# Strassen's seven products in three of five column groups of each feed-forward layer, with the sums of weights on GpSimd

## The chip, the cores and the metric

One core of a Trainium2 chip runs the whole program in one launch. The metric is the device time in microseconds, the median of several runs. The engines are TensorE (PE in the rows, its weight loads PEld), VectorE (DVE), ScalarE (ACT), GpSimd (POOL) and SyncE (SP), which here issues the weight transfers.

## The reference, cut to what matters

Two blocks of a transformer over 256 tokens of 1024 features, in float32, have three feed-forward layers of the same shape, with 2816 hidden columns:

```
def swiglu(h, w1, w3, w2):
    return (jax.nn.silu(h @ w1) * (h @ w3)) @ w2      # h [256, 1024], w1 and w3 [1024, 2816], w2 [2816, 1024]
```

The second block's layer is the same with other names (w_ffn_gate, w_ffn_up, w_ffn_down). `h` is the normed input; the kernel multiplies by the norm's factor of a row only after the product. The change touches `h @ w1` and `h @ w3`, which this document calls the first projections.

## The kernel before, in words

**Products.** A float32 product is made of three passes on TensorE: each operand is split into a high and a low part of 12 bits, and high*high, high*low and low*high are summed in PSUM (`mm3`, L196 to L198). The normed tokens stand still, 128 of them by 128 features at a time (`n["hi"]`, `n["lo"]`, tiles xT_hi and xT_lo), and 512 columns of weights move past them.

**Weights.** All weights go once through SBUF, in the order of use (`Stream`). A load brings 2048 words of each partition (1 MB: four chunks of 128 rows by 512 columns) into one of four w_raw buffers, by a transfer that SP issues. A piece is half a load: two chunks of 128 rows by 512 columns. For each piece ScalarE makes the high part (L141, w_raw to w_hi) and VectorE the low part (L142, w_raw less w_hi, to w_lo); both inputs of L142 lie in SBUF. `advance` keeps `AHEAD = 4` pieces split ahead of the one in use, and there are five buffers for each part.

**The feed-forward layer** (`ffn`, L410). The 2816 columns are cut in five groups of 512 and one of 256. A group calls `proj` for w1 and then for w3. Each `proj` takes four pieces; with each piece it makes six matrix instructions for the first 128 tokens and six for the others, into two PSUM banks. So a group has 8 pieces and 96 matrix instructions. When a bank is full, `gate` (L433, ScalarE, silu from PSUM to sg) or `up` (L438, VectorE, PSUM times factor times sg, to hid) empties it. Then `turn` transposes hid on TensorE, eight blocks of 128 by 128 in two parts, and each part is split to hT_hi (L204, ScalarE) and hT_lo (L205, VectorE) for the last projection (`outproj`, L362), which comes after all groups.

**Order.** The order of each engine's work is that in which the Python program issues it. Side work are generators; a `tick` comes after every six large matrix instructions and runs what is due (`turn` waits 2 ticks before each of its parts), then calls `advance`. `finish` ticks until given tasks are done. GpSimd has only the small steps of the norms and of head factors (`inv_sqrt`, L225 to L230, on tiles of 1 to 8 columns, `norm_s`, L261) and four copies (L729).

Of the kernel before, what the change touches and what calls it, by code (L numbers as in the profile page):

```python
# [23 lines left out]
F32 = mybir.dt.float32  # L24
# [5 lines left out]
P = 128  # L30
# [24 lines left out]
# columns of the constants, in three parts (always needed, first block, second block)  # L55
# [5 lines left out]
# Ticks that the tensor engine's share of a task waits for the other engines' (see Kernel.spawn).  # L61
# [48 lines left out]
class Stream:  # L110
    """Weights in the order of their use: loads run ahead, splits run ahead of the products."""

    def __init__(self, nc, raw, hi, lo, ahead_load, ahead_split):
        self.nc, self.raw_p, self.hi_p, self.lo_p = nc, raw, hi, lo
        self.al, self.asp = ahead_load, ahead_split
        self.slots, self.pieces = [], []
        self.raws, self.parts = {}, {}
        self.i = self.loaded = self.split = 0

    def add(self, w, k0, kc, c0, n):  # L120
        """Rows k0*P .. (k0+kc)*P of w, n columns from c0: one load, split by as many row chunks as a piece holds."""
        self.slots.append((w, k0, kc, c0, n))
        step = PIECE // n
        for k in range(0, kc, step):
            self.pieces.append((w, k0 + k, min(step, kc - k), c0, n, len(self.slots) - 1, k))

    def _load(self, i):
        w, k0, kc, c0, n = self.slots[i]
# [4 lines left out]
        self.raws[i] = v  # L133

    def _split(self, i):
        nc = self.nc
        w, k0, kc, c0, n, slot, k = self.pieces[i]
        raw = self.raws[slot][:, k * n:(k + kc) * n]
# [4 lines left out]
        self.parts[i] = (hi.rearrange("p (k n) -> p k n", n=n), lo.rearrange("p (k n) -> p k n", n=n))  # L143

    def advance(self, limit=10 ** 9):
        want = min(len(self.pieces) - 1, self.i + self.asp - 1, limit)
        slot = min(len(self.slots), self.pieces[min(self.i, len(self.pieces) - 1)][5] + self.al)
        while self.loaded < max(slot, self.pieces[want][5] + 1):
            self._load(self.loaded)
            self.loaded += 1  # L150
        while self.split <= want:
            self._split(self.split)
            self.split += 1

    def take(self, w, k0, c0):
        if self.i not in self.parts:
            self.advance()
        spec = self.pieces[self.i]
        assert spec[0] is w and spec[1] == k0 and spec[3] == c0, (spec[1:], k0, c0)
        got = self.parts.pop(self.i)  # L160
        self.i += 1
        return spec[2], got


class Kernel:
    def __init__(self, ctx, tc, a, out):
# [3 lines left out]
        self.raw = pool("raw", 4)  # L170
# [21 lines left out]
    def mm3(self, out, a, b, start=False, stop=False):  # L192
        """out += a.T @ b, both split."""
# [6 lines left out]
    def evac_split(self, hi, lo, src, scale=None):  # L200
        """hi + lo = src * scale."""
# [8 lines left out]
    def split(self, hi, lo, src):  # L210
        """hi + lo = src, all in SBUF."""
# [7 lines left out]
    def inv_sqrt(self, out, ss, n, eps, width):  # L219
        """out = (ss / n + eps) ** -0.5"""  # L220
# [19 lines left out]
    def norm_piece(self, n, gcol, h, c):  # L240
        """x * g, transposed and split, for half h of the tokens and half c of the features; its squares' sum."""
# [27 lines left out]
    # Work beside the large products: generators, that yield after how many ticks to go on. A tick comes after  # L269
    # every six large products, so what a task asks of the other engines is done when the tensor engine needs it.  # L270
# [852 lines left out]
```

## Time and profile before

| what | value |
|---|---|
| median of three runs | 1030.45 us (1028.41 to 1030.77) |
| profiled execution, span | 1027.8 us |
| PE busy | 1013.2 us, 99% |
| DVE busy | 628.4 us, 61% |
| ACT busy | 546.8 us, 53% |
| POOL busy | 64.1 us, 6% |
| mean DMA rate | 170 GB/s |

The span runs from the first to the last instruction of the profiled execution; its own time with what lies around the span isn't given apart, and the median of the runs is 2.65 us above the span. The page gives each engine's busy time, then the chain of work that ended last: what each step waited for, followed back from the last instruction. Busy time of PE counts pipelined instructions, so the rate is read from starts, not from durations.

### The profile page before, as it was taken

The page shows a single profiled execution, that of the slowest core. Times are in us where ns is not written, and L with a number is a line of the kernel's source. Part 1 is how long each engine was busy: PE and PEld are TensorE (multiplying, and loading weights), DVE is VectorE, ACT ScalarE, POOL GpSimd, SP SyncE. Part 2 cuts the span into 40 slices and gives each one's busy share as a digit, 9 for nine tenths or more (in the row PEclk, how much of TensorE's full clock was granted, in tenths as well). Part 3 has the DMA queues.
Part 4 walks back from the last instruction along what each step waited for, and adds up shares of the span by engine and source line. Part 5 has one row for each costly group of instructions (what it writes and reads, how often), then busy time and mean ns, then how long its engine had stood idle before and what let it go on. Part 6 is the DMA issues. An engine that isn't in the chain of part 4 may idle for free.

```text
span 1027.8 us, 13120 instructions
## 1 busy us (share of the span) xinstructions
PE 1013.2 (99%) x5126; PEld 846.9 (82%) x5126; DVE 628.4 (61%) x892; ACT 546.8 (53%) x820; POOL 64.1 (6%) x167
## 2 busy tenths in 40 slices
PE   7999999999999999999999999999999999999998
PEld 6887888898888998788888888888887888888886
DVE  5977655554475877655555466666677665555542
ACT  7666545443366776644444366675444464444431
POOL 2320000000010000200000015000020010000000
PEclk9999999999999999999999999999999999999999
DMA  9543655555555323465655545355534546555541
GB/s 308 179 140 106 217 193 170 199 168 201 164 198 170 106 100 104 140 202 172 202 169 190 176 163 205 124 194 171 198 123 167 182 145 226 181 195 175 183 144 42
DMA packets 82638, 174.50 MB, mean 170 GB/s; under 512 B 2960, under 2 KB 19984, under 8 KB 82576
## 3 DMA queue, kind: packets, MB, share of 16 engines
q1 hardware_dynamic: 82288, 173.57, 49.9%
q8 instruction: 40, 0.66, 0.3%
q14 instruction: 22, 0.18, 0.1%
q10 hardware_dynamic: 288, 0.09, 0.0%
HBM read 172.60 MB, written 1.05 MB: 169 GB/s over the span
## 4 chain that ended last, share of the span: by engine, by line
PE 93%; DVE 3%; POOL 2%; issue 1%; ACT 1%; DMA 1%; SPq 0%; DVEq 0%; ACTq 0%
PE acc L362 27%; PE acc L196 18%; PE acc L198 18%; PE acc L197 18%; PE misc L217 4%; PE z L196 1%; POOL is_y L226 1%; PE z L198 1%; PE z L197 1%; PE misc L197 1%; DMA x<-in_x_dram 1%; PE misc L196 1%; PE misc L198 1%; PE z L821 1%; PE z L807 0%
## 5 line engine op out<-in xcount | busy, mean ns | idle before, releaser
L142 DVE TENSOR_TENSOR w_lo<-w_raw,w_hi 128x1024 fp32r<-128x1024 f32 (+1 forms) x323 | 392.7, 1222 | 301.2 <-ACT w_hi L141 300.8
L141 ACT CAST w_hi<-w_raw 128x1024 fp32r<-128x1024 f32 (+1 forms) x323 | 337.3, 1050 | 354.8 <-PE acc L198 228.5
L196 PE MATMUL acc<-w_hi,xT_hi 128*128 128x512 f32 (+2 forms) x1008 | 372.1, 370 | 0.0
L197 PE MATMUL acc<-w_lo,xT_hi 128*128 128x512 f32 (+2 forms) x1008 | 366.7, 364 | 0.0
L198 PE MATMUL acc<-w_hi,xT_lo 128*128 128x512 f32 (+2 forms) x1008 | 366.5, 364 | 0.0
L198 PEld LDWEIGHTS acc<-w_hi,xT_lo 128*128 128x128 f32 x1008 | 190.2, 189 | 30.3
L196 PEld LDWEIGHTS acc<-w_hi,xT_hi 128*128 128x128 f32 x1008 | 190.3, 189 | 29.1 <-ACT xT_hi L207 0.9
L197 PEld LDWEIGHTS acc<-w_lo,xT_hi 128*128 128x128 f32 x1008 | 190.5, 189 | 28.0
L362 PE MATMUL acc<-w_lo,hT_hi 128*128 128x512 f32 x264 | 104.6, 396 | 0.0
L362 PE MATMUL acc<-w_hi,hT_hi 128*128 128x512 f32 x264 | 104.4, 395 | 0.0
L362 PE MATMUL acc<-w_hi,hT_lo 128*128 128x512 f32 x264 | 86.7, 395 | 0.0
L362 PEld LDWEIGHTS acc<-w_hi,hT_hi 128*128 128x128 f32 x264 | 49.8, 189 | 11.3
L362 PEld LDWEIGHTS acc<-w_hi,hT_lo 128*128 128x128 f32 x264 | 49.7, 188 | 11.3
L362 PEld LDWEIGHTS acc<-w_lo,hT_hi 128*128 128x128 f32 x264 | 49.7, 188 | 11.1
L261 POOL TENSOR_TENSOR norm_s<-norm_ss 128x1 f32<-128x1 f32 x12 | 3.8, 313 | 611.8 <-ACT junk L257 611.8
L208 DVE SCALAR_TENSOR_TENSOR xT_lo<-misc,gains,xT_hi 128x128 fp32r<-128x128 f32 (+1 forms) x84 | 28.0, 353 | 22.6 <-ACT xT_hi L207 22.5
L207 ACT ACTIVATE xT_hi<-misc,gains 128x128 fp32r<-128x128 f32 (+1 forms) x84 | 29.0, 371 | 11.5 <-DVE xT_lo L208 9.0
L433 ACT ACTIVATE sg<-acc,norm_rstd 128x512 f32<-128x512 f32 (+1 forms) x36 | 23.6, 655 | 18.1 <-PE acc L198 17.9
L396 DVE TENSOR_TENSOR x<-acc,x 128x512 f32<-128x512 f32 x24 | 16.5, 690 | 14.1 <-PE acc L362 13.7
L438 DVE SCALAR_TENSOR_TENSOR hid<-acc,norm_rstd,sg 128x512 f32<-128x512 f32 (+1 forms) x36 | 23.9, 700 | 0.5 <-PE acc L198 0.5
L226 POOL TENSOR_TENSOR is_y<-is_v,mhalf 128x1 f32<-128x1 f32 (+2 forms) x24 | 23.8, 993 | 2.0
L257 ACT ACTIVATE junk<-x 128x512 f32<-128x512 f32 x24 | 15.2, 632 | 16.4 <-DVE x L396 14.7
(266 smaller groups left out, 973.8 us busy)
## 6 DMA issues: line engine op xcount, KB each, us to landing
w_raw<-in_ffn_w_dram SPq DMA_DIRECT2D x66, 1024.0 KB, 5.0
w_raw<-in_w_in_dram SPq DMA_DIRECT2D x26, 1024.0 KB, 5.0
w_raw<-in_od_w_qkv_dram SPq DMA_DIRECT2D x12, 1024.0 KB, 5.2
w_raw<-in_w_ffn_gate_dram SPq DMA_DIRECT2D x11, 1024.0 KB, 5.1
w_raw<-in_w_ffn_up_dram SPq DMA_DIRECT2D x11, 1024.0 KB, 5.0
w_raw<-in_w_ffn_down_dram SPq DMA_DIRECT2D x11, 1024.0 KB, 4.8
w_raw<-in_ev_w_in_dram SPq DMA_DIRECT2D x5, 1024.0 KB, 7.8
w_raw<-in_ev_w_out_dram SPq DMA_DIRECT2D x4, 1024.0 KB, 7.0
```

Source lines behind the costliest of these rows:

```text
L141: nc.scalar.copy(hi, raw)
L142: nc.vector.tensor_sub(lo, raw, hi.bitcast(F32))
L196: nc.tensor.matmul(out, ah, bh, start=start, stop=False, skip_group_check=True)
L197: nc.tensor.matmul(out, ah, bl, start=False, stop=False, skip_group_check=True)
L198: nc.tensor.matmul(out, al, bh, start=False, stop=stop, skip_group_check=True)
L207: nc.scalar.mul(hi, src, scale)
L208: nc.vector.scalar_tensor_tensor(lo, src, scale, hi.bitcast(F32), op0=OP.mult, op1=OP.subtract)
L217: self.nc.tensor.transpose(out, in_, self.ident)
L226: nc.gpsimd.tensor_tensor(y, v, self.mhalf[:, :width], op=OP.pow)
L362: mm = lambda a, b, start, stop: self.nc.tensor.matmul(o, a, b, start=start, stop=stop, skip_group_check=True)
L433: nc.scalar.activation(s[:, :m], acc[:, :m], AF.Silu, scale=n["rstd"][:, h:h + 1])
L438: nc.vector.scalar_tensor_tensor(t[:, :m], acc[:, :m], n["rstd"][:, h:h + 1], sg[h][:, :m], op0=OP.mult, op1=OP.mult)
```

## The change: what it does

The two projections of one group are one product: the tokens' matrix, cut in four quarters (two halves of 128 tokens by two halves of 512 features), times a matrix with 512 columns of w1 on the left and the same 512 of w3 on the right, also in four quarters of 512 rows by 512 columns (b11, b12, b21, b22). Before, that took eight products of quarters. In three groups of each layer (the second, third and fifth) it now takes seven, in Winograd's arrangement of Strassen's scheme: x1 = a11 b11 and w = a12 b21, whose sum is the upper left quarter of the result, one product of a sum of tokens with b22 as it lies, one of a22 with a sum of weights, and three of sums with sums. Each product takes two pieces and twelve matrix instructions. A group so has 14 pieces and 84 matrix instructions, where it had 8 and 96.

The sums of weights are made on GpSimd (`_sum`): four for a group, each an addition of two tiles of 128 by 2048 words. The first three take a buffer of a pool of two (w_sum), the fourth is written over the second. A sum may be issued up to 12 pieces ahead of its use, if its sources have been issued as loads or sums and a buffer is free. The sums of tokens (`token_sums`) are made once for a layer, after its first group, on VectorE with copies on ScalarE, from xT_hi and xT_lo. Products add up in PSUM where they can; where a partial sum is used twice, ScalarE copies the bank (`snap`), and VectorE adds or subtracts (`result`).

The weight loads have five buffers in place of four, and a load is issued as soon as the load five before it has been split and summed. In the retention layer the split scores lie in other tiles, and head 3 waits for head 0's end. All else in the diff is comments.

```
+RING = 5
+SUMS = 2
+SUMS_AHEAD = 12
...
+    def add_block(self, wl, cl, wr, cr):
+        h = KD // 2
+        b11 = self._load_of(wl, 0, h, cl, 512)
+        b12 = self._load_of(wr, 0, h, cr, 512)
+        b22 = self._load_of(wr, h, h, cr, 512)
+        b21 = self._load_of(wl, h, h, cl, 512)
+        s1 = self._sum_of(b11, b12)
+        s2 = self._sum_of(s1, b22)
+        s3 = self._sum_of(b12, b22)
+        s4 = self._sum_of(s2, b21, over=True)
+        for q, src in ((1, b11), (2, b21), (5, s1), (6, s2), (3, b22), (7, s3), (4, s4)):
+            for k in range(0, h, 2):
+                self._piece(src, k * 512, 2, 512, (wl, q, k, cl))
...
+    def _may_load(self):
+        j = self.loaded
+        return j < len(self.loads) and (j < self.ring or self.loads[j - self.ring]["users"] == 0)
...
+    def _sum(self):
...
+            s["tile"] = self.sum_p.tile([P, SLOT], F32, name="w_sum")
...
+        self.nc.gpsimd.tensor_tensor(s["tile"], x["tile"], y["tile"], op=OP.add)
...
+    FF_GROUPS = ((0, 512, False), (512, 512, True), (1024, 512, True), (1536, 512, False), (2048, 512, True), (2560, 256, False))
...
+    def token_sums(self, n, pool, tmp, out):
...
+        def difference(dst, x, y):
+            nc.vector.tensor_sub(dst, f(*x, "hi"), f(*y, "hi"))
+            nc.vector.tensor_sub(e, f(*x, "lo"), f(*y, "lo"))
+            nc.vector.tensor_add(dst, dst, e)
+
+        def done(which, src):
+            hi, lo = out[which]
+            nc.scalar.copy(hi, src)
+            nc.vector.tensor_sub(lo, src, hi.bitcast(F32))
+
+        difference(s, (1, 0), (1, 1))
+        done(5, s)
+        yield 2
+        nc.vector.tensor_sub(s, s, f(0, 0, "hi"))
+        nc.vector.tensor_sub(s, s, f(0, 0, "lo"))
+        done(6, s)
+        yield 2
+        nc.vector.tensor_add(s, s, f(0, 1, "hi"))
+        nc.vector.tensor_add(s, s, f(0, 1, "lo"))
+        done(3, s)
+        yield 2
+        difference(d, (0, 0), (1, 0))
+        done(7, d)
+
+    def block(self, n, sums, wl, c0, wr, snap, result):
...
+                    self.mm3(acc, left[q](k + kk), (wh[:, kk], wl_[:, kk]), start=start and k + kk == 0, stop=k + kk == KD // 2 - 1)
+                if k + kc < KD // 2:
+                    self.tick()
...
+        x = self.ps_acc()
+        product(x, 1, True)
+        after(snap, "x1", x)
+        w = self.ps_acc()
+        product(w, 2, True)
+        after(result, 0, 0, w)
+        z = self.ps_acc()
+        product(z, 5, True)
+        after(snap, "z", z)
+        product(x, 6, False)
+        after(snap, "x2", x)
+        product(z, 3, False)
+        after(result, 1, 0, z)
+        product(x, 7, False)
+        after(snap, "x3", x)
+        v = self.ps_acc()
+        product(v, 4, True)
+        after(result, 0, 1, v)
...
+                def snap(what, acc):
+                    nc.scalar.copy(home[what], acc)
+                    if what == "x3":
+                        nc.vector.tensor_sub(hid[1], hid[1], sg[1])
+
+                def result(side, h, acc):
+                    if side == 0:
+                        nc.vector.tensor_add(sg[h], acc, sg[h])
+                        nc.scalar.activation(sg[h], sg[h], AF.Silu, scale=n["rstd"][:, h:h + 1])
+                    else:
+                        nc.vector.tensor_sub(hid[h], acc, hid[h])
+                    if side == 1 or h == 1:
+                        nc.vector.scalar_tensor_tensor(hid[h], hid[h], n["rstd"][:, h:h + 1], sg[h], op0=OP.mult, op1=OP.mult)
...
+            for c0, m, block in self.FF_GROUPS:
+                if block:
+                    self.finish([made])
+                hid = by_block(c0) if block else plain(c0, m)
+                if not made:
+                    made = self.spawn(self.token_sums(n, f2, lambda i: f2.tile([P, 512], F32, name=("sg0", "sg1", "hid0")[i]), sums))
                 last = self.spawn(turn(c0, m, hid))
...
             def ret_head(j):
+                while j >= 3 and rets[j - 3] in self.live:
+                    yield 1
...
-                sh = se2.tile([P, 384], F32R, name="ret_sh")
-                sl = se2.tile([P, 384], F32R, name="ret_sl")
+                sh, sl = splits[j % 3]
```

## Rows read from the trace of the kernel before

**Rows 1.** The profile's page: busy time by engine; chain that ended last, by engine.

```profile
PE 1013.2 (99%) x5126; PEld 846.9 (82%) x5126; DVE 628.4 (61%) x892; ACT 546.8 (53%) x820; POOL 64.1 (6%) x167
...
PE 93%; DVE 3%; POOL 2%; issue 1%; ACT 1%; DMA 1%; SPq 0%; DVEq 0%; ACTq 0%
```

**Rows 2.** Busy time by stretch: first projections of the three layers, columns named above.

```profile
core 0: us, PE busy (x) PEld busy (x) DVE busy (x) ACT busy (x) POOL busy (x), PEclk, DMA share, GB/s
...
98.60:224.20 125.60, 125.60 (x621) 106.02 (x621) 71.86 (x77) 63.50 (x81) 2.07 (x7) 1.00 0.58 193
...
419.50:545.00 125.50, 125.50 (x619) 104.88 (x619) 71.01 (x79) 63.15 (x83) 3.36 (x8) 1.00 0.55 185
...
836.50:962.30 125.80, 125.80 (x623) 106.21 (x622) 72.25 (x78) 62.79 (x79) 2.06 (x7) 1.00 0.57 193
```

**Rows 3.** The same view, one group of 512 columns, between two starts of L438.

```profile
165.87:188.61 22.74, 22.74 (x105) 18.80 (x105) 12.32 (x13) 10.66 (x12) 0.00 (x0) 1.00 0.56 184
```

**Rows 4.** Timeline of PE, 163 to 168 us (start, duration); instructions follow one another.

```profile
164.80 0.39 PE L196 MATMUL acc<-w_hi,xT_hi 128*128 128x512 f32 x1
...
167.97 0.39 PE L198 MATMUL acc<-w_hi,xT_lo 128*128 128x512 f32 x1
```

**Rows 5.** Instruction groups by shape, 143.14 to 188.61 us: busy us, mean ns, idle before.

```profile
L142 DVE TENSOR_TENSOR w_lo<-w_raw,w_hi 128x1024 fp32r<-128x1024 f32 x17 | 20.8, 1225 | 22.3 <-ACT w_hi L141 22.3
L141 ACT CAST w_hi<-w_raw 128x1024 fp32r<-128x1024 f32 x16 | 16.8, 1053 | 22.2 <-PE acc L198 22.2
...
L438 DVE SCALAR_TENSOR_TENSOR hid<-acc,norm_rstd,sg 128x512 f32<-128x512 f32 x4 | 2.8, 744 | 0.0
L433 ACT ACTIVATE sg<-acc,norm_rstd 128x512 f32<-128x512 f32 x4 | 2.8, 690 | 1.9 <-PE acc L198 1.9
L205 DVE TENSOR_TENSOR hT_lo<-misc,hT_hi 128x512 fp32r<-128x512 f32 x4 | 2.7, 684 | 0.0
...
L204 ACT CAST hT_hi<-misc 128x512 fp32r<-128x512 f32 x4 | 2.3, 579 | 0.0
```

**Rows 6.** Instruction groups of DVE over the span: 128x512, both inputs in SBUF.

```profile
L976 DVE TENSOR_TENSOR a<-a,b 128x512 f32<-128x512 f32 x4 | 2.7, 682 | 0.0
```

**Rows 7.** Timeline of DVE, 48 to 58 us.

```profile
48.43 1.22 DVE L142 TENSOR_TENSOR w_lo<-w_raw,w_hi 128x1024 fp32r<-128x1024 f32 x1
...
51.95 1.22 DVE L142 TENSOR_TENSOR w_lo<-w_raw,w_hi 128x1024 fp32r<-128x1024 f32 x1
53.09 0.74 DVE L208 SCALAR_TENSOR_TENSOR qT<-misc,gq,qT 128x512 fp32r<-128x512 f32 x1
53.75 2.35 DVE L142 TENSOR_TENSOR w_lo<-w_raw,w_hi 128x1024 fp32r<-128x1024 f32 x2
```

**Rows 8.** Timeline of POOL, the same stretch.

```profile
48.60 1.10 POOL L225 TENSOR_SCALAR is_v<-hn_ss 128x8 f32<-128x8 f32 x1 [5.92 <-DVE hn_ss L454]
49.79 1.64 POOL L226 TENSOR_TENSOR is_y<-is_v,mhalf 128x8 f32<-128x8 f32 x1
...
52.07 1.15 POOL L229 TENSOR_SCALAR is_t<-is_t 128x8 f32<-128x8 f32 x1
53.31 0.20 POOL L230 TENSOR_TENSOR rq<-is_t,is_y 128x8 f32<-128x8 f32 x1
...
53.88 3.71 POOL L226 TENSOR_TENSOR is_y<-is_v,mhalf 128x8 f32<-128x8 f32 x1
```

**Rows 9.** Instruction groups of POOL, 28 to 33 us.

```profile
L729 POOL CAST vp<-vp 128x128 fp32r<-128x128 f32 x3 | 0.9, 292 | 9.5 <-ACT vp L207 9.2 <-DVE vp L208 0.3
```

**Rows 10.** Instruction groups of POOL, 603 to 606 us.

```profile
L228 POOL TENSOR_TENSOR is_t<-is_t,is_v 128x1 f32<-128x1 f32 x1 | 0.2, 191 | 0.1
```

**Rows 11.** Instruction groups of POOL, 626 to 628 us.

```profile
L228 POOL TENSOR_TENSOR is_t<-is_t,is_v 128x8 f32<-128x8 f32 x1 | 0.2, 204 | 0.1
```

**Rows 12.** Timeline of DVE, 176 to 190 us, the end of a group.

```profile
187.47 1.22 DVE L142 TENSOR_TENSOR w_lo<-w_raw,w_hi 128x1024 fp32r<-128x1024 f32 x1 [1.49 <-ACT w_hi L141]
188.61 1.40 DVE L438 SCALAR_TENSOR_TENSOR hid<-acc,norm_rstd,sg 128x512 f32<-128x512 f32 x2
```

More of the change, by code (lines that the diff above doesn't have):

```diff
@@ L110, with __init__ @@
 class Stream:
-    def __init__(self, nc, raw, hi, lo, ahead_load, ahead_split):
+    def __init__(self, nc, raw, hi, lo, ring, sum_ring, ahead_split, ahead_sum):
         self.nc, self.raw_p, self.hi_p, self.lo_p = nc, raw, hi, lo
[L115 to L118, printed above, removed]
+        self.sum_p = None
+        self.ring, self.sum_ring, self.asp, self.asum = ring, sum_ring, ahead_split, ahead_sum
+        self.loads, self.sums, self.pieces = [], [], []
+        self.buffers = []
+        self.parts = {}
+        self.taken = 0
+        self.i = self.loaded = self.summed = self.split = 0
@@ new lines, in _source, with _load_of, _sum_of @@
+    def _source(self, **kw):
+        return dict(users=0, tile=None, **kw)
+    def _load_of(self, w, k0, kc, c0, n):
+        s = self._source(spec=(w, k0, kc, c0, n), words=kc * n)
+        self.loads.append(s)
+        return s
+    def _sum_of(self, x, y, over=False):
+        s = self._source(xy=(x, y), words=x["words"], first=None, over=over, heir=None)
+        x["users"] += 1
+        y["users"] += 1
+        if over:
+            x["heir"] = s
+        else:
+            self.buffers.append(s)
+        self.sums.append(s)
+        return s
@@ L129, in _load @@
+    def _load(self):
+        s = self.loads[self.loaded]
+        w, k0, kc, c0, n = s["spec"]
         t = self.raw_p.tile([P, SLOT], F32, name="w_raw")
@@ L132, in _load, with _may_sum, _split @@
                                w[k0 * P:(k0 + kc) * P, c0:c0 + n].rearrange("(k p) n -> p k n", p=P))
-        self.raws[i] = v
-    def _split(self, i):
+        s["tile"] = v
+        self.loaded += 1
+    def _may_load(self):
+        j = self.loaded
+        return j < len(self.loads) and (j < self.ring or self.loads[j - self.ring]["users"] == 0)
+    def _may_sum(self):
+        j = self.summed
+        if self.sum_p is None or j >= len(self.sums) or any(x["tile"] is None for x in self.sums[j]["xy"]):
+            return False
+        s = self.sums[j]
+        if s["over"]:
+            return s["xy"][0]["users"] == 1
+        if self.taken < self.sum_ring:
+            return True
+        last = self.buffers[self.taken - self.sum_ring]
+        while last["users"] == 0 and last["heir"] is not None:
+            last = last["heir"]
+        return last["users"] == 0
+    def _sum(self):
+        s = self.sums[self.summed]
+        x, y = s["xy"]
+        if s["over"]:
+            s["tile"] = x["tile"]
+        else:
+            s["tile"] = self.sum_p.tile([P, SLOT], F32, name="w_sum")
+            self.taken += 1
+        self.nc.gpsimd.tensor_tensor(s["tile"], x["tile"], y["tile"], op=OP.add)
+        x["users"] -= 1
+        y["users"] -= 1
+        self.summed += 1
+    def _split(self):
         nc = self.nc
-        w, k0, kc, c0, n, slot, k = self.pieces[i]
-        raw = self.raws[slot][:, k * n:(k + kc) * n]
+        src, off, kc, n, key = self.pieces[self.split]
+        raw = src["tile"][:, off:off + kc * n]
         hi = self.hi_p.tile([P, PIECE], F32R, name="w_hi")[:, :kc * n]
@@ new lines, in block, with product, after @@
+    def block(self, n, sums, wl, c0, wr, snap, result):
+        plain = lambda k0, h: lambda k: tuple(n[p][:, k0 + k, h * P:(h + 1) * P] for p in ("hi", "lo"))
+        summed = lambda i: lambda k: tuple(t[:, k] for t in sums[i])
+        left = {1: plain(0, 0), 2: plain(4, 0), 4: plain(4, 1), **{i: summed(i) for i in (3, 5, 6, 7)}}
+        def product(acc, q, start):
+            for k in range(0, KD // 2, 2):
+                kc, (wh, wl_) = self.st.take(wl, q, k, c0)
+                for kk in range(kc):
+                    self.mm3(acc, left[q](k + kk), (wh[:, kk], wl_[:, kk]), start=start and k + kk == 0, stop=k + kk == KD // 2 - 1)
+                if k + kc < KD // 2:
+                    self.tick()
+        def after(f, *args):
+            self.run(f(*args))
+            self.tick()
+        x = self.ps_acc()
[16 more added lines that the diff above has]
+        after(result, 0, 1, v)
@@ L425, in turn, with plain @@
                     self.evac_split(hh[:, k:k + 2, :], hl[:, k:k + 2, :], tp.rearrange("p (k t) -> p k t", t=T))
-            for c0 in range(0, FF, 512):
-                m = min(512, FF - c0)
+            def plain(c0, m):
                 sg, hid = [], []
```

93 lines of the change are left out of this document (63 added, 30 removed).

## Prediction, on record before the changed kernel ran

> **What bounds the kernel now.** I read the page first: PE is busy 99% of the span and makes 93% of the chain that ended last, DVE 3% [rows 1]. So PE's stream of matrix instructions sets the time, and POOL is nearly free (64.1 us). Next the stretches: the first projections of the three layers take 125.6, 125.5 and 125.8 us, PE busy throughout, the granted clock 1.00, its higher level (2.4 GHz) [rows 2]. Then one group of 512 columns: 22.74 us, in which DVE is busy 12.32 and ACT 10.66 us [rows 3]. The reader is to see that this slack, some 10 us of DVE, belongs to a group of 8 pieces. Last the PE timeline: 15 matrix instructions start between 164.80 and 167.97 us, so 3.17 / 14 = 0.2264 us apart [rows 4]; 96 of them are 21.74 us, and the other 1.0 us of the group is the eight transposes.
>
> **What PE saves.** 12 instructions fewer in each of nine groups: 12 x 0.2264 = 2.72 us a group, 24.5 us in all. A changed group costs PE 84 x 0.2264 + 1.0 = 20.0 us.
>
> **What DVE gets.** A changed group has 14 pieces where there were 8, and each wants one L142 and one L141. On DVE, by rows 5 for the same kinds and rows 6 for two inputs in SBUF: 14 x 1.225 = 17.15; two additions and one subtraction from PSUM, 3 x 0.684 = 2.05 (as L205); the subtraction after x3, 0.68; two products as L438, 2 x 0.744 = 1.49; two L205, 1.37. Together 22.7 us in 22 instructions. Instructions back to back overlap a little: two L142 take 2.35 us, so the second adds 1.13 and not 1.22 [rows 7], and L438 starts 1.14 us after L142 [rows 12]. Less 0.09 for each: 20.8 us. ACT: 14 x 1.053 + four copies and two casts of turn at 0.579 + two silus at 0.690 = 19.6 us [rows 5]. So even alone DVE takes 20.8 us of a group of which PE wants 20.0: the cover of rows 3 is gone, because a piece now feeds six instructions (1.36 us) where it fed twelve. Only 1.9 us a group could be won against 22.74.
>
> **Sums of tokens.** After the first group of a layer DVE makes 14 instructions of 128 x 512 with both inputs in SBUF: 14 x (0.682 - 0.08) = 8.4 us [rows 6], and in each of the four `done` it waits for ACT's copy, about 0.6 us (0.579 in rows 5): 10.8 us in all. They stand on DVE ahead of the split of piece 5 of the next group. PE has four pieces ahead (4 x 1.36) and the transposes (1.0), 6.4 us, and then waits.
>
> **Second and third group together, without GpSimd in the way.** From the end of the first group DVE has: its last L438 0.66, the sums of tokens 10.8, turn 1.2, 24 pieces (the first four are split) x 1.13 = 27.1, the other work of the second group 5.0, that of the third before its last piece 2.5. This is 47.3 us; PE's last six instructions make it 48.7, against 2 x 22.74 = 45.5 before: 3.2 us worse. The fifth group follows a plain one and takes 20.8: 1.9 better. A layer loses 1.3 us, the three layers 4, even if sums cost nothing.
>
> **The sums on GpSimd.** None of this size is in the trace. Their length: an addition or product of two inputs takes POOL 191 ns at 1 column and 204 at 8 [rows 10, 11], 1.86 ns an element or 4.0 us at 2048; the copy of 128 columns takes 292 ns [rows 9], some 101 ns over the 191, so 0.8 ns an element of one input, 1.8 us at 2048 with one and 3.4 with two. Ends: 1.8 and 4.0 us. I take 3.4, from the row with the most columns, which is the nearest. The Trainium skill ("GPSIMD Engine Reference", section "Elementwise — side-by-side cycle accounting") states 4497 ns for just such an addition; no row here has one, and by it the time below would be 1142 us.
>
> What they do to DVE is the question. POOL's is_v at 48.60, usually 0.20 us (as L230 at 53.31), takes 1.10 and ends at 49.70, just after the L142 that ran from 48.43 to 49.65; L229 at 52.07 takes 1.15 and ends at 53.22, after the L142 that ended at 53.17 [rows 7, 8]. The pow at 53.88 takes 3.71 where the one at 49.79 took 1.64: it sits out two L142 in a row. But L230 at 53.31 runs in 0.20 beside an L208 that reads PSUM. So an instruction of POOL that reads SBUF and one of DVE with two inputs in SBUF do not run together: the later one waits for the other's end. The rows show it for POOL waiting; I take it that DVE waits as well, for a whole sum. The Trainium skill says so: "SBUF — State Buffer", section "Who interferes with whom", has DVE's second input and POOL share a read port that the first to start holds for its whole instruction. The trace agrees for the one direction, and has no POOL instruction long enough for the other.
>
> L142, the sums of tokens and L438's successor all have two inputs in SBUF, so nearly all of DVE's time in a changed group is closed to sums. What stands behind a waiting L142 on DVE: the next splits, the additions that empty PSUM, turn. PE waits for all of them after four pieces (5.4 us).
>
> Of a layer's twelve sums, four fall in plain groups, two in the first and two in the fourth: `SUMS_AHEAD = 12` lets s1 and s2 go there, while s3 needs the buffer that s1 leaves. There 12.32 + 2 x 3.4 = 19.1 us still fits under 22.74 [rows 3], so these cost nothing. Six fall between the first group's end and the third's: 6 x 3.4 = 20.4 us. Two fall in the fifth: 6.8.
>
> **The sum.** A layer: 3.2 + 20.4 - 1.9 + 6.8 = 28.5 us; three layers 85.5 us. On the profiled execution's span of 1027.8 that is 1113; the runs' median is 2.65 above the span, so I forecast 1116 us. I count no relief from DVE's work on PSUM beside a sum: it's 5 x 0.60 = 3.0 us in a group, at most 27 us in nine, and DVE works in order. With sums of 1.8 us: 3 x (3.2 + 10.8 - 1.9 + 3.6) = 47, so 1078, and with all the relief 1051. With 4.0 us: 3 x (3.2 + 24 - 1.9 + 8) = 100, so 1130.
>
> **Costed at nothing.** The copies of PSUM banks on ACT have a product in between (2.7 us), as long as ACT isn't behind. Transfers: as many bytes, at a share of 0.56 of the DMA engines [rows 3]; the SP queue runs a buffer further ahead, and may hold back the retention constants, which are asked for a whole projection before their use. Head 3 of the retention waits at most a tick more, six instructions, 1.4 us.
>
> **Rivals.**
> *A, the port is no matter* (POOL waits for gaps, DVE never waits for it): then the sums run under PE's and DVE's other work, and what is left is the 4 us above, 1034 us. Part of the sum of tokens may slip into waits of DVE, so 1020 to 1040. For it: DVE's L142 show 1.22 us also beside POOL. Against: those POOL instructions read eight elements, and a DVE that is 20.8 us busy in 20.0 leaves no gaps; then the sum, and PE after it, waits.
> *B, PE stays the bound* (faster): if DVE and ACT find room by overlapping more than back-to-back rows show, all 24.5 us come, 1006 us. It decides from under 20.0 us of DVE per group; 22.7 us of plain durations speak against it.
> *C, more than the sum* (slower still): sums and splits wait for one another in a chain. The next group's s1 takes the buffer that s4 leaves, so it can't start before the last L142 of the group has read it, and that L142 waits for s4. If at each of the nine groups one sum, its L141 and its L142 stand bare, with nothing of DVE's beside, that is 9 x (3.4 + 1.05 + 1.22) = 51 us on top, 1167 us. PE would also idle for microseconds at a time, where the granted clock might leave 1.00; no row shows that.
> That the products don't save is no rival: their count is in the code.
>
> **How the numbers follow.** The forecast (1050 to 1135) has 0.70, A 0.13, B 0.07, C 0.10. A's own range splits: 0.05 faster, 0.04 same, 0.04 slower. A measurement of this kernel can tell 0.3%, some 3 us, from no change. Faster: B and part of A, 0.12. Same: 0.04. Slower: 0.84. The range runs from 1026, in A, to 1150, between the forecast's upper end and C; about 0.16 is left out.
>
> **What would show it.** PE's instructions fall by 108 and the granted clock stays. The second and third group take over 30 us each, the fifth about 28, the fourth 23. L142's spans there are either long (DVE held by a sum) or leave gaps of a sum's length, and POOL's sums show 3 to 5 us when alone, more when they wait. ACT's and DVE's idle time in a changed group follows w_sum. The prediction is wrong if L142 keeps 1.22 us and short gaps while a sum runs beside it: then A or B. It's wrong in size if a sum takes under 2 us.

## The result, and the profile after

The changed kernel takes 1138.18 us in the median of four runs (1136.97 to 1139.04). The kernel before takes 1030.01 us in the same session, so the ratio is 1.1053, with an interval of 1.104 to 1.1066. The change costs 108 us. The forecast was 1116 us.

The page after, to be read against [rows 1]: busy time by engine, then the chain by engine.

```profile
PE 1037.7 (91%) x5018; PEld 851.7 (75%) x5018; DVE 862.6 (76%) x1024; ACT 625.3 (55%) x922; POOL 241.8 (21%) x203
...
PE 76%; DVE 13%; issue 6%; ACT 2%; POOL 1%; DMA 1%; SPq 0%; DVEq 0%; ACTq 0%
```

TensorE issues 108 instructions fewer, as counted, and is busy longer. The span is 1136.1 us and the mean granted clock 0.961. TensorE's share of the chain falls from 93 to 76%, VectorE's rises from 3 to 13%, and "issue" (time in which the engine waited for nothing that the profile shows) from 1 to 6%. Two rows of the list of waits (total, times, longest) say where TensorE stands still; the list of before has nothing like them. A matrix instruction and its weight load stand still at the same time, so the two rows don't add up:

```profile
PEld acc L287 <- DVE w_lo L225: 90.2, 29, 6.2
...
PE acc L287 <- DVE w_lo L225: 77.8, 25, 5.7
```

L225 of the changed kernel is the split that was L142; L213 is the new sum. Nearly all of the loss lies in the first projections: they take 161.8, 160.7 and 162.1 us in the three layers, against 125.4, 126.7 and 125.4 before, measured in both from the layer's start to the first product of hT (so the numbers differ a little from [rows 2]). That is 36.4, 34.0 and 36.7 us, 107.1 together. Layer 1 by groups, the first from the layer's start, each to the start of the group's last instruction on hid, columns as in [rows 2]. The first group, the second with the third, the fourth, the fifth, the last:

```profile
99.30:125.50 26.20, 24.38 (x102) 19.50 (x101) 22.55 (x23) 14.96 (x26) 12.11 (x9) 0.93 0.56 188
125.50:203.80 78.30, 56.20 (x205) 42.66 (x204) 74.41 (x57) 41.42 (x50) 30.19 (x6) 0.85 0.33 111
203.80:223.10 19.30, 19.26 (x89) 15.63 (x88) 19.27 (x12) 9.09 (x11) 10.85 (x2) 1.00 0.54 182
223.10:251.50 28.40, 24.63 (x114) 19.69 (x113) 27.99 (x23) 19.16 (x23) 9.19 (x2) 0.94 0.46 151
251.50:261.30 9.80, 9.80 (x84) 9.76 (x84) 7.11 (x10) 5.00 (x8) 0.00 (x0) 1.00 0.76 288
```

The second and third group take 78.3 us where two groups took 45.4. VectorE is "busy" for 74.41 of them, with 57 instructions. The forms over the whole run, with mean ns, explain it; the row of w_lo from w_raw answers to [rows 5], that of xs (the sums of tokens) to [rows 6]:

```profile
L225 DVE TENSOR_TENSOR w_lo<-w_raw,w_hi 128x1024 fp32r<-128x1024 f32 x302 | 447.8, 1500 | 159.8 <-ACT w_hi L224 159.5
L225 DVE TENSOR_TENSOR w_lo<-w_sum,w_hi 128x1024 fp32r<-128x1024 f32 x72 | 118.8, 1682 | 0.8 <-ACT w_hi L224 0.8
L522 DVE TENSOR_TENSOR xs<-sg,xs 128x512 fp32r<-128x512 f32 x12 | 20.9, 1766 | 0.2
L626 DVE TENSOR_TENSOR sg<-acc,sg 128x512 f32<-128x512 f32 x18 | 12.2, 679 | 0.0
```

Before, the split had 1225 ns, and an addition of 128 x 512 with both inputs in SBUF 682. Of these rows only those with both inputs in SBUF grew; L626, which adds a PSUM bank to a copy and so reads one input from PSUM, still has 679. The waiting shows inside the instruction's span and not as idle time, so a busy share can't tell it from work. On GpSimd the sum has these rows:

```profile
L213 POOL TENSOR_TENSOR w_sum<-w_sum,w_raw 128x2048 f32<-128x2048 f32 x18 | 90.8, 5046 | 37.8 <-issue 28.6 <-DVE w_lo L225 6.9 <-DMA w_raw<-in_ffn_w_dram 1.9
L213 POOL TENSOR_TENSOR w_sum<-w_raw 128x2048 f32<-128x2048 f32 x18 | 88.8, 4936 | 302.1 <-DMA w_raw<-in_ffn_w_dram 149.0 <-DVE w_lo L225 78.7 <-ACT xs L521 59.1
```

The lock can be read off one stretch of 13 us. GpSimd's timeline (start, duration):

```profile
106.25 4.61 POOL L213 TENSOR_TENSOR w_sum<-w_raw 128x2048 f32<-128x2048 f32 x1 [0.31 <-issue]
110.94 5.44 POOL L213 TENSOR_TENSOR w_sum<-w_sum,w_raw 128x2048 f32<-128x2048 f32 x1
```

And VectorE's:

```profile
108.51 3.43 DVE L225 TENSOR_TENSOR w_lo<-w_raw,w_hi 128x1024 fp32r<-128x1024 f32 x1 [0.59 <-ACT w_hi L224]
111.87 0.34 DVE L298 SCALAR_TENSOR_TENSOR xT_lo<-misc,gains,xT_hi 128x128 fp32r<-128x128 f32 x1
112.13 6.46 DVE L225 TENSOR_TENSOR w_lo<-w_raw,w_hi 128x1024 fp32r<-128x1024 f32 x2
```

The first sum ends at 110.86. The split that came at 108.51 ends 1.08 us later, at 111.94: it waited for the whole sum. The second sum, issued at 110.94, meets that split and takes 0.9 us longer than a bare one, ending at 116.38. The next two splits end at 118.59, which is 2.2 us after it; bare they take 2.35 [rows 7]. Each waits for the other's end. A sum that starts while VectorE runs no instruction with two inputs in SBUF takes 4.54 to 4.64 us. A later stretch has a third kind beside them (GpSimd's row first, then two of VectorE's):

```profile
153.30 5.48 POOL L213 TENSOR_TENSOR w_sum<-w_raw 128x2048 f32<-128x2048 f32 x1 [4.62 <-DVE w_lo L225]
154.22 0.68 DVE L629 TENSOR_TENSOR hid<-acc,hid 128x512 f32<-128x512 f32 x1
154.82 5.04 DVE L225 TENSOR_TENSOR w_lo<-w_sum,w_hi 128x1024 fp32r<-128x1024 f32 x1
```

L629 reads one input from PSUM and runs its bare 0.68 us beside the sum; the split behind it sits the sum out. It is so all through this trace: of the VectorE instructions that started inside one of the 36 sums, the 35 with both inputs in SBUF all ended after it, and the 23 with an input in PSUM took 0.34 to 0.69 us. In the chain of work such held time goes under "issue". A row of VectorE's timeline, and a row of the chain that lies inside it, while a sum runs from 134.10 to 139.05:

```profile
133.98 5.62 DVE L522 TENSOR_TENSOR xs<-sg,xs 128x512 fp32r<-128x512 f32 x2
134.75 4.78 issue
```

### The profile page after: what moved, and what is told of

Its sections match the earlier page's. It is cut to its first block, busy times and chain, and to the rows that moved or that the text cites. A ratio compares the mean times of both kernels' runs of the same rounds, so it can differ in the third digit from the quotient of the medians.

```text
span 1136.1 us, 13298 instructions
## 1 busy us (share of the span) xinstructions
PE 1037.7 (91%) x5018; PEld 851.7 (75%) x5018; DVE 862.6 (76%) x1024; ACT 625.3 (55%) x922; POOL 241.8 (21%) x203
## 3 DMA queue, kind: packets, MB, share of 16 engines
q1 hardware_dynamic: 82288, 173.57, 44.5%
## 4 chain that ended last, share of the span: by engine, by line
PE 76%; DVE 13%; issue 6%; ACT 2%; POOL 1%; DMA 1%; SPq 0%; DVEq 0%; ACTq 0%
PE acc L452 25%; PE acc L287 14%; PE acc L288 14%; PE acc L286 14%; DVE w_lo L225 9%; PE misc L307 4%; PE z L286 1%; ACT w_hi L224 1%; PE z L288 1%; PE z L287 1%; POOL is_y L316 1%; DMA x<-in_x_dram 1%; DVE hT_lo L295 1%; PE misc L288 1%; PE misc L287 1%
## 5 line engine op out<-in xcount | busy, mean ns | idle before, releaser
L225 DVE TENSOR_TENSOR w_lo<-w_raw,w_hi 128x1024 fp32r<-128x1024 f32 (+1 forms) x305 | 451.0, 1496 | 162.5 <-ACT w_hi L224 162.2
L287 PE MATMUL acc<-w_lo,xT_hi 128*128 128x512 f32 (+2 forms) x828 | 303.6, 367 | 20.1 <-DVE w_lo L225 20.0
L286 PE MATMUL acc<-w_hi,xT_hi 128*128 128x512 f32 (+2 forms) x828 | 305.6, 370 | 0.0
L288 PE MATMUL acc<-w_hi,xT_lo 128*128 128x512 f32 (+2 forms) x828 | 300.9, 363 | 3.1 <-DVE xT_lo L298 3.1
L288 PEld LDWEIGHTS acc<-w_hi,xT_lo 128*128 128x128 f32 x828 | 159.3, 192 | 26.4 <-DVE xT_lo L298 3.9
L213 POOL TENSOR_TENSOR w_sum<-w_raw 128x2048 f32<-128x2048 f32 x18 | 88.8, 4936 | 302.1 <-DMA w_raw<-in_ffn_w_dram 149.0
L287 PE MATMUL acc<-w_lo,xs 128*128 128x512 f32 x144 | 69.8, 485 | 57.8 <-DVE w_lo L225 57.8
L224 ACT CAST w_hi<-w_sum 128x1024 fp32r<-128x1024 f32 x72 | 74.0, 1050 | 84.6 <-PE acc L288 51.8
L225 DVE TENSOR_TENSOR w_lo<-w_sum,w_hi 128x1024 fp32r<-128x1024 f32 x72 | 118.8, 1682 | 0.8 <-ACT w_hi L224 0.8
L213 POOL TENSOR_TENSOR w_sum<-w_sum,w_raw 128x2048 f32<-128x2048 f32 x18 | 90.8, 5046 | 37.8 <-issue 28.6
L286 PE MATMUL acc<-w_hi,xs 128*128 128x512 f32 x144 | 66.9, 473 | 2.2 <-ACT xs L521 1.8
L288 PE MATMUL acc<-w_hi,xs 128*128 128x512 f32 x144 | 66.9, 465 | 0.0
```

The costliest lines, as they stand in the source:

```text
L213: self.nc.gpsimd.tensor_tensor(s["tile"], x["tile"], y["tile"], op=OP.add)
L224: nc.scalar.copy(hi, raw)
L225: nc.vector.tensor_sub(lo, raw, hi.bitcast(F32))
L286: nc.tensor.matmul(out, ah, bh, start=start, stop=False, skip_group_check=True)
L287: nc.tensor.matmul(out, ah, bl, start=False, stop=False, skip_group_check=True)
L288: nc.tensor.matmul(out, al, bh, start=False, stop=stop, skip_group_check=True)
```

## The experiments

Each was timed beside the kernel before, which had 1030.16 us with the first four, 1029.27 with e5, e6, e7 and e9, and 1029.5 with the last two. The theory called "port" is the prediction's: a sum that reads SBUF and an instruction of VectorE with two inputs in SBUF shut each other out. Its rivals are "load" (VectorE just has too much to do) and "chain" (sums and splits wait for each other's buffers).

**e1: GpSimd writes as many words, and reads none.** The sums' values are left out.

```diff
-        self.nc.gpsimd.tensor_tensor(s["tile"], x["tile"], y["tile"], op=OP.add)
+        self.nc.gpsimd.memset(s["tile"], 1.0)
```

> The sums of weights are left out: in place of each addition GpSimd fills the same buffer with a constant, so it writes SBUF and reads nothing, and no longer waits for loads. All else of the change stays: 14 pieces, sums of tokens, buffers. Theory 'port' (a sum and a VectorE instruction with two SBUF inputs exclude each other for the whole instruction): the holding is gone, L225 goes back to 1.22 us, time 1034 us (1015 to 1045). Theory 'load' (14 pieces and the sums of tokens on VectorE make the loss): over 1100 us, little changed from 1138. Theory 'chain' (buffers and order of sums, each waiting for splits): 1090 to 1120, as the waits for buffers stay.

Measured: 1022.48 us, ratio 0.993 (0.9915 to 0.9944): faster than the kernel before. The same forms as above:

```profile
L225 DVE TENSOR_TENSOR w_lo<-w_raw,w_hi 128x1024 fp32r<-128x1024 f32 x302 | 364.8, 1221 | 184.0 <-ACT w_hi L224 183.6
L225 DVE TENSOR_TENSOR w_lo<-w_sum,w_hi 128x1024 fp32r<-128x1024 f32 x72 | 85.7, 1218 | 3.2 <-ACT w_hi L224 2.9
...
L213 POOL MEMSET w_sum<- 128x2048 f32 x36 | 65.1, 1815 | 349.2 <-DVE w_lo L225 150.9 <-PE misc L288 117.5 <-ACT xs L521 75.4
```

The split is back at 1.22 us; summed over its 374 instances that is 566.6 less 450.5, 116 us of VectorE's span. The time falls by 115.7. That the two agree so well is chance: L522 falls from 1766 to 684 ns as well, and VectorE's whole busy time by 131.7 us (862.6 to 730.9). "Load" (over 1100 us) has fallen, since the splits and the sums of tokens all stayed, and so has "chain" (1090 to 1120). What stays open is that this instruction is also shorter, 1.8 against 4.55 us, which e9 takes up, and that it waits for no loads and holds no load's buffer. The second isn't parted by a run with GpSimd; the change's list of waits has GpSimd waiting for loads of these layers' weights, but none of ScalarE's or VectorE's splits.

**e2: the sums of tokens left out.** The products take plain quarters of the tokens, and `token_sums` isn't spawned.

```diff
-        left = {..., **{i: summed(i) for i in (3, 5, 6, 7)}}
+        left = {..., 3: plain(0, 1), 5: plain(0, 0), 6: plain(4, 0), 7: plain(4, 1)}
...
-                    made = self.spawn(self.token_sums(...))
+                    made = True
```

> The sums of tokens are left out (plain quarters stand in their place), the sums of weights on GpSimd stay. 'Port': VectorE loses 10.8 us of work a layer where it is the bound, 32 us in all, some more for sums that ran into them: 1095 to 1110 us. 'Load': the same 32 us or more. 'Chain': nothing of it is on the chain of sums, 1125 to 1138.

Measured: 1098.40 us, ratio 1.067 (1.0654 to 1.0686), inside the range of "port". "Load" expected as much, so this run speaks only against "chain" (1125 to 1138). The sums of tokens are worth 39.8 us beside sums that read, and the sums of weights still take most of the loss.

**e3: both edits at once.**

> Both left out: sums of weights as constants written by GpSimd, no sums of tokens. What is left is 84 matrix instructions and 14 splits a group. By the ledger of the prediction VectorE needs 20.8 us a group and TensorE 20.0 against 22.74: nine groups win 1.9 us each, 1013 us (1005 to 1022). If TensorE is the bound again it is 1006. 'Load' without the port: 1030 or more.

Measured: 1005.89 us, ratio 0.9766 (0.9752 to 0.9781), 24.3 us less than before: TensorE's whole saving, which the prediction put at 24.5. Of the outcomes named it is the one with TensorE as the bound; "load" without the port (1030 or more) has fallen. A layer's first projections take 117.3, 118.5 and 117.2 us. A stretch of 44.5 us in the second and third group, columns as in [rows 2]:

```profile
120.00:164.50 44.50, 44.50 (x206) 36.70 (x205) 43.36 (x47) 38.58 (x46) 14.53 (x8) 1.00 0.44 152
```

TensorE is busy throughout and VectorE for 43.36 us, 97%: it just fits. So the four variants give a table (us). Reading sums cost 92.5 without the sums of tokens and 115.7 with them; the sums of tokens cost 16.6 without reading sums and 39.8 with them.

| | GpSimd writes only | GpSimd adds |
|---|---|---|
| no sums of tokens | 1005.89 | 1098.40 |
| sums of tokens | 1022.48 | 1138.18 |

**e4: the sums on the engine that is already full.**

```diff
-        self.nc.gpsimd.tensor_tensor(s["tile"], x["tile"], y["tile"], op=OP.add)
+        self.nc.vector.tensor_tensor(s["tile"], x["tile"], y["tile"], op=OP.add)
```

> The sums of weights are made on VectorE, not on GpSimd, in the same order and with the same buffers. 'Port': the bound is the sum of both engines' time on the port, and VectorE adds two tiles of 2048 in about 2.2 us (twice L142 less its fixed part) where GpSimd takes 4.5; a layer is 3.2 + 6 x 2.2 - 1.9 + 2 x 2.2 = 18.9 us over, the time 1087 us (1070 to 1100): faster than on the idle engine. 'Load' or 'chain': VectorE only gets more, 1138 to 1200.

Measured: 1067.22 us, ratio 1.0364 (1.0346 to 1.0381). That is 71 us less than with the sums on GpSimd, and 20 less than "port" said, below its range of 1070 to 1100; its sum holds the prediction's ledger of VectorE, which e1 shows to be 12 us too dear. "Load" and "chain" (1138 or more) are further off. The sum takes 2.28 us here, and VectorE is full (62.47 of 63.00 us in the second and third group):

```profile
L213 DVE TENSOR_TENSOR w_sum<-w_sum,w_raw 128x2048 f32<-128x2048 f32 x18 | 41.1, 2285 | 0.1
```
```profile
120.00:183.00 63.00, 50.31 (x206) 38.58 (x206) 62.47 (x64) 41.39 (x50) 0.00 (x0) 0.95 0.37 124
```

Thirty-six sums of 2.28 us take 82 us of VectorE, and the time is 44.7 us above that of e1, where nothing is added. A sum of 4.55 us on GpSimd keeps VectorE from its two-input work for twice as long as it would take there itself, whenever it has such an instruction to do, and the same sums cost 115.7 us over e1.

**e5: rival C's chain cut.** The third sum goes over b12, so the next group's first sum doesn't wait for the buffer that s4 leaves.

```diff
-        s3 = self._sum_of(b12, b22)
+        s3 = self._sum_of(b12, b22, over=True)
```

`_may_load` then also waits for the sum that lies in the buffer.

> The third sum (b12 + b22) is written over b12, which no product reads as it lies, so it needs no buffer: the first three sums can be made a group ahead and the next group's first sum no longer waits for the last of this one. Sums stay on GpSimd. 'Port': the same 36 sums and the same work on VectorE, only in another order; a third sum of each block now falls in a plain group, whose room on VectorE (22.74 less 12.3) two sums of 4.5 us had filled: 1125 to 1145. 'Chain': the sums no longer wait for one another, some 50 us are won, 1075 to 1100.

Measured: 1139.34 us, ratio 1.1067 (1.1052 to 1.1083), no different from the change (1.104 to 1.1066). This chain of buffers isn't what costs. The loss moved with the sums: in layer 1 the first group takes 30.2 us (26.4 in the change) and the fourth 23.7 (19.3), the second and third 75.1 (78.3) and the fifth 24.3 (28.4), and the total stays.

**e6: TensorE kept at work.** Two more instructions for each piece, 28 a changed group, into a bank that nobody reads.

```diff
+                for _ in range(2):
+                    self.nc.tensor.matmul(self.idle, left[q](k)[0], wh[:, 0], start=True, stop=True, skip_group_check=True)
```

> After each piece of a changed group TensorE makes two more matrix instructions into a bank that nothing reads, 28 a group, 0.45 us a piece at the higher clock. They fill part of the waits, so that the granted clock may stay up. If the lower clock (0.961 mean over the span) costs time: the clock rises to 0.98 or more, and the time falls by 10 to 30 us, 1108 to 1128. If VectorE and the sums set the time whatever the clock: 1132 to 1142. If the extra work only adds: up to 9 x 6.3 = 57 us more, 1195.

Measured: 1146.32 us (1143.44 to 1148.73), ratio 1.1135 (1.1117 to 1.1152). The mean clock rises from 0.961 to 0.983, and the time rises too, by 8 us, so that only the last of the outcomes named (up to 1195) contains it. In the second and third group, from 123.2 to 198.1 us in this run, VectorE is at its end:

```profile
123.20:198.10 74.90, 61.79 (x252) 48.29 (x252) 74.90 (x58) 40.02 (x49) 30.35 (x6) 0.93 0.36 121
```

Over the whole the filler wins nothing. In this stretch, where the clock was lowest, the three layers take 75.0, 75.8 and 75.0 us against 78.3, 78.5 and 77.5 in the change; the fifth group (31.7 against 28.4) and the fourth (20.9 against 19.3) lose more than that. The filler adds 252 instructions of its own, so what the lower clock costs in the changed kernel isn't told apart by it.

**e7: two changed groups a layer, sums on VectorE.** If VectorE's time in the plain groups pays for the sums, they fit. The third and fifth group are changed, the second is plain; a sum may be made 20 pieces ahead, one in a tick.

```diff
-SUMS = 2
-SUMS_AHEAD = 12
+SUMS = 3
+SUMS_AHEAD = 20
...
-    FF_GROUPS = (..., (512, 512, True), (1024, 512, True), (1536, 512, False), (2048, 512, True), (2560, 256, False))
+    FF_GROUPS = (..., (512, 512, False), (1024, 512, True), (1536, 512, False), (2048, 512, True), (2560, 256, False))
```

Besides, the sums as in e4, s3 over b12 as in e5, s4 with a buffer of its own, and four buffers for loads (the constants then come in by a buffer of w_lo).

> A version from the findings: two changed groups of a layer (the third and fifth), each behind a plain one; sums on VectorE, with three buffers and the third sum over b12, so that all four of a group are made in the plain group before it, at most one for a tick; four load buffers. A layer saves 2 x 2.72 us of TensorE, 16.3 in all. VectorE has some 10.4 us of room in a plain group and the sums want 4 x 2.29 = 9.2; the sums of tokens (10.8) run in the second group beside the first sums. If all is hidden: 1014 us. If the sums of tokens and the first sums don't fit: 1020 to 1030. Above 1031 if VectorE's backlog reaches TensorE as before.

Measured: 1021.89 us, ratio 0.9926 (0.9913 to 0.994), of the 16 us on offer a little under half. The second and the third group:

```profile
121.40:144.70 23.30, 23.30 (x109) 19.24 (x108) 23.27 (x27) 10.62 (x14) 0.00 (x0) 1.00 0.41 129
144.70:170.80 26.10, 24.92 (x110) 19.55 (x109) 25.46 (x27) 21.95 (x26) 0.00 (x0) 1.00 0.57 185
```

VectorE has no room between 121 and 144 us, where the sums of tokens meet the first sums of weights, and TensorE loses 1.2 us in the group after. A load that lands late has a part in it: the chain of work waits for one from 140.67 to 145.78, and the fourth sum and the splits wait with it.

**e9: GpSimd as long as with the sum, without reading.** Three writes in place of the one of e1, 5.4 us of GpSimd for each sum.

```diff
-        self.nc.gpsimd.tensor_tensor(s["tile"], x["tile"], y["tile"], op=OP.add)
+        for _ in range(3):
+            self.nc.gpsimd.memset(s["tile"], 1.0)
```

> As the first experiment (sums of weights left out, GpSimd writes a constant), but with three fills for each sum, so that GpSimd is busy 3 x 1.8 = 5.4 us, longer than an addition, and still reads nothing. 'Port', as far as it is reading that excludes: VectorE is not held, L225 stays at 1.22 us, time 1022 to 1035 (the third fill may come late for its split). If GpSimd's length is what matters, whether it reads or not: 1100 to 1140.

Measured: 1035.40 us, ratio 1.006 (1.0047 to 1.0074), 0.4 us above the range of "port". One timeline of each engine, GpSimd's and VectorE's, in the second and third group:

```profile
129.95 21.82 POOL L214 MEMSET w_sum<- 128x2048 f32 x12 [16.83 <-ACT xs L522]
153.20 22.03 POOL L214 MEMSET w_sum<- 128x2048 f32 x12 [1.43 <-DVE w_lo L226]
...
135.79 2.35 DVE L226 TENSOR_TENSOR w_lo<-w_raw,w_hi 128x1024 fp32r<-128x1024 f32 x2
138.06 2.35 DVE L226 TENSOR_TENSOR w_lo<-w_sum,w_hi 128x1024 fp32r<-128x1024 f32 x2
```

GpSimd writes without a break from 129.95 to 151.77, and the splits (L226 here) run through it at their bare 2.35 us for two; no split of this run takes over 1.23. A GpSimd that is busy for longer than in the change thus costs 13 us over e1. ScalarE waits 24.8 us in all for a late w_sum here, about as long as in the change (29.2), and 0.9 in e1. The other 103 us, from 1035.4 to 1138.2, come with the reading. The Trainium skill has this asymmetry too: "SBUF — State Buffer", section "Who interferes with whom", says that two SBUF inputs on VectorE contend with a GpSimd instruction that reads SBUF and not with one that only writes. Both halves of it are now in rows of this case.

**e10: the order of the groups.** As e7, with the group of 256 second, so that the sums of tokens get a plain stretch to themselves, and spawned half a group earlier.

```diff
-    FF_GROUPS = ((0, 512, False), (512, 512, False), (1024, 512, True), (1536, 512, False), (2048, 512, True), (2560, 256, False))
+    FF_GROUPS = ((0, 512, False), (2560, 256, False), (512, 512, False), (1024, 512, True), (1536, 512, False), (2048, 512, True))
```

> The version with two changed groups and sums on VectorE, with the room moved to where it was short: in that version VectorE was full from the second group's start (23.3 of 23.3 us) to the third's end, since the sums of tokens and the first four sums of weights met there. Now the group of 256 columns comes second and the first changed group fourth, and the sums of tokens begin in the middle of the first group. Order: plain 512, plain 256, plain 512, changed, plain 512, changed. VectorE has about 5 + 6 + 10 us of room ahead of the first changed group, and 20 are wanted. If that was what cost the rest: 1014 to 1018 us. If VectorE is short in the changed groups themselves, or the loads come late with four buffers: 1019 to 1023.

Measured: 1016.10 us (1015.91 to 1018.63), ratio 0.9874 (0.9857 to 0.9891): 13.4 us faster than the kernel before, 122 faster than the change. The four groups of 512 that end the layer:

```profile
133.40:156.10 22.70, 22.70 (x103) 18.78 (x102) 19.80 (x16) 10.61 (x12) 0.00 (x0) 1.00 0.49 156
156.10:178.40 22.30, 22.30 (x102) 18.23 (x101) 21.20 (x23) 19.05 (x23) 0.00 (x0) 1.00 0.54 186
178.40:199.90 21.50, 21.50 (x100) 17.77 (x99) 20.57 (x18) 10.77 (x12) 0.00 (x0) 1.00 0.58 203
199.90:221.40 21.50, 21.50 (x99) 17.59 (x98) 20.98 (x23) 18.47 (x22) 0.00 (x0) 1.00 0.54 194
```

TensorE is busy in every one, and VectorE's load is even, 19.8 to 21.2 us. Two groups a layer save 6 x 2.72 = 16.3 us on TensorE, and 13.4 of them arrive.

**e8: e7 with the sums back on GpSimd.**

```diff
-        self.nc.vector.tensor_tensor(s["tile"], x["tile"], y["tile"], op=OP.add)
+        self.nc.gpsimd.tensor_tensor(s["tile"], x["tile"], y["tile"], op=OP.add)
```

> The version with two changed groups of a layer behind plain ones (order and buffers as in the run of 1021.89 us), but with its 24 sums on GpSimd. It differs from that run in the engine of one instruction alone. 'Port': a plain group now has 12.3 + 4 x 4.55 = 30.5 us of VectorE's and GpSimd's time on the port against 22.74, so the sums spill into the changed group; some 8 us for each of the six pairs, less what VectorE's instructions on PSUM use beside them: 1050 to 1075 us. If an idle GpSimd is good for sums once they have a plain group each to run in: 1010 to 1022.

Measured: 1091.45 us, ratio 1.0599 (1.0578 to 1.0619); above the range, so "port" was too mild here. One word in the code is worth 69.6 us, 2.9 us for each of 24 sums.

```profile
L218 POOL TENSOR_TENSOR w_sum<-w_sum,w_raw 128x2048 f32<-128x2048 f32 x12 | 60.8, 5066 | 34.5 <-DMA w_raw<-in_ffn_w_dram 23.7 <-DMA w_raw<-in_w_ffn_gate_dram 10.4 <-DMA w_raw<-in_w_ffn_up_dram 0.2
```
```profile
L230 DVE TENSOR_TENSOR w_lo<-w_raw,w_hi 128x1024 fp32r<-128x1024 f32 x320 | 442.2, 1397 | 182.2 <-ACT w_hi L229 181.9
```

The sums of this form take 5.07 us, and the splits of loads grow to 1.40 us, while those of sums stay at 1.22, in a schedule that wins 7 us with the sums on VectorE. The two kernels differ in nothing but the engine, and both read.

## Why the prediction was right, and where it was off

**Right: the mechanism and the side.** The forecast rested on a sum and a VectorE instruction with two inputs in SBUF shutting each other out both ways, of which the trace of before showed only one. The rows at 108.51 and 110.94 show both. Rival A (the port no matter) fell with e9 against the change, rival B (TensorE stays the bound) with the change itself.

**Misread: a row against the second way.** The prediction read the trace of before as showing that an instruction of GpSimd that reads SBUF and one of VectorE with two inputs there do not run together, and as having none of GpSimd's long enough to show VectorE waiting. The pow at 49.79 speaks against both: it runs for 1.64 us [rows 8], and a split that starts inside it takes its bare time (VectorE's timeline):

```profile
50.16 1.22 DVE L142 TENSOR_TENSOR w_lo<-w_raw,w_hi 128x1024 fp32r<-128x1024 f32 x1
```

So not every instruction of GpSimd that reads SBUF holds VectorE for its whole length. The additions of 2048 columns do; why this one, on eight columns, doesn't, no run here shows.

**Right: TensorE's saving.** 12 x 0.2264 us in each of nine groups gave 24.5 us; e3 returns 24.3.

**Mis-sized: the length of a sum.** The step took 3.4 us from a copy of 128 columns with one input [rows 9], doubled, and 4.0 as its upper end. Bare it is 4.55 us, outside both ends. The Trainium skill ("GPSIMD Engine Reference", section "Elementwise — side-by-side cycle accounting") had 4497 ns, within 2% of it, and the prediction's sentence on it gave 1142 us. A two-input addition grows from 191 ns at one column to 4.55 us at 2048, 2.13 ns a column; the row with two inputs at eight columns [rows 11], which gave the 4.0, was nearer than the copy. In the prediction's own formula 4.55 us gives 3.2 + 6 x 4.55 - 1.9 + 2 x 4.55 = 37.7 us a layer, against 36.4, 34.0 and 36.7 measured. This one term is 8 x 1.15 = 9.2 us a layer, 27.6 in all, more than the miss of 22.

**Too dear: VectorE's ledger.** It had a changed group at 20.8 us of VectorE and the sums of tokens at 10.8, so that a layer lost 1.3 us before any sum. In e1 the layers win 2.7, 2.7 and 2.5 us, some 11.9 us in all the other way. There VectorE ends the last split of the third group 43.0 us after the first group's end, where the step had 47.3, with the same 24 splits in between; and e1 less e3 puts the sums of tokens at 5.5 us a layer. They don't stand in one row ahead of the next split as the step had it: in e1 splits come between them, VectorE doesn't stand idle for ScalarE's copies, and TensorE doesn't wait out the whole row.

**Where in the layer.** The second and third group lose 32.9 us in layer 1 and the fourth gains 3.5 (16 of its 105 instructions now lie ahead of its boundary, since VectorE's last instruction on hid comes later), so 29.4 belong to the sums' six in that stretch: 23.6 were forecast, 30.5 by a sum of 4.55 us. The fifth with the last loses 3.2; 4.9 were forecast.

**Wrong: "these cost nothing", of the four sums in plain groups.** The two in the fourth group do cost nothing (TensorE is busy 19.26 of its 19.30 us). But the first group of a layer takes 3.7, 1.4 and 4.9 us longer, where 12.32 + 2 x 3.4 us was to fit under 22.74. The sum of busy times did fit, and TensorE waited all the same: at 110.05 it stops for L298 (the low part of the normed tokens, L208 before), which stands on VectorE behind the split held by the sum. Room over a whole group doesn't cover one split of 3.43 us right in front of what TensorE wants next.

**Wrong: "the granted clock stays".** It falls to a mean of 0.961; in the rows below (next section but one) after TensorE has waited. What it costs was neither forecast nor shown apart. Rival C's chain of buffers fell in e5.

**Luck in the number.** The sums' length was 27.6 us too short and the first groups add 10.0, while the ledger was 11.9 too dear. These three come to 25.7 against the 21.6 by which the layers missed (107.1 less 85.5), so that the forecast stands as near as it does because the errors partly cancel; where the remaining 4 us lie isn't shown.

**Rows to watch.** The prediction said that the split's spans would be long rather than followed by gaps if VectorE is held; they are (1.50 and 1.68 us on the mean). A sum was to take 3 to 5 us alone and more when it waits; it takes 4.54 to 4.64, and up to 5.52. The prediction said over 30 us for the second and third group each (39), about 28 for the fifth (28.4) and 23 for the fourth (19.3, for the reason above).

## What to carry to other kernels

An engine that shows 6% busy isn't free for work that reads SBUF, if a neighbour on the path reads two SBUF inputs in most of its instructions: price its work as a stop of the neighbour, for long instructions such as these for the whole length of each. The same sums were 71 us cheaper on the engine that was already the tightest, and 69.6 in another schedule; that it does them in half the time is the likely reason, but no run changes the length alone. And a saving on the bound that adds load to the second engine pays as far as that load can be spread over stretches with room: two changed groups a layer won 7.4 us, and 13.4 with the groups in another order, where three, two of them adjacent, lost 37 even with the cheaper sums (that run also had other buffers).

## What the hardware showed that was not expected

A write of 128 x 2048 words on GpSimd takes 1.81 us and holds no split of VectorE's (e1, e9), while an addition of the same size takes 4.55 and holds every two-input instruction that starts inside it.

TensorE's granted clock can fall to the lower level (1.2 GHz) after a wait that is short beside a layer. In the changed kernel's TensorE timeline, around a wait of 1.82 us in the first group, with a row of the stretch at the lower level (columns as in [rows 2]) behind it:

```profile
112.26 0.50 PE L288 MATMUL acc<-w_hi,xT_lo 128*128 128x512 f32 x1 [1.82 <-DVE xT_lo L298]
112.60 0.40 PE L286 MATMUL acc<-w_hi,xT_hi 128*128 128x512 f32 x1
112.83 0.39 PE L287 MATMUL acc<-w_lo,xT_hi 128*128 128x512 f32 x1
...
113.68 0.63 PE L287 MATMUL acc<-w_lo,xT_hi 128*128 128x512 f32 x1
114.11 0.63 PE L288 MATMUL acc<-w_hi,xT_lo 128*128 128x512 f32 x1
...
116.67 0.43 PE L288 MATMUL acc<-w_hi,xT_lo 128*128 128x512 f32 x1
116.94 0.40 PE L286 MATMUL acc<-w_hi,xT_hi 128*128 128x512 f32 x1
117.17 0.40 PE L287 MATMUL acc<-w_lo,xT_hi 128*128 128x512 f32 x1
```
```profile
113.68:116.67 2.99, 2.99 (x8) 2.31 (x7) 2.99 (x1) 0.80 (x1) 2.70 (x1) 0.50 0.88 321
```

Starts are 0.23 us apart right after the wait, 0.43 from 113.68 on, where the granted clock is 0.50, and 0.23 again from 116.94, after TensorE had run without a gap since 112.26. In the second and third group the mean is 0.85, and 205 instructions are busy for 56.20 us where as many take 46.42 in e1, at 1.00:

```profile
121.30:170.90 49.60, 46.42 (x205) 36.02 (x204) 49.09 (x58) 40.77 (x50) 14.52 (x8) 1.00 0.37 126
```
